# Router of tiles 4 and 5 behind the last output product, one pass of largest values for four tiles, VectorE in program order

## The chip, the core and the metric

The kernel runs on one core of a Trainium2 chip. The time is device microseconds (us) from the start to the end of one execution. TensorE multiplies matrices and transposes by multiplying with an identity; VectorE and ScalarE do the elementwise work; GpSimd (POOL in the rows) does small copies and the indirect gathers; the sync queue (SP) issues nearly all DMAs. In the rows VectorE is DVE, ScalarE is ACT, TensorE is PE, its loads of stationary operands are PEld.

## What is computed

One layer over 1024 tokens of width 1024, in eight tiles of 128 tokens (0 to 7), in float32 throughout: a mixer (differential attention of four heads beside a short convolution, then an output projection), a residual with norms, and an expert-choice mixture of 16 experts. This is the part that matters here:

```python
cap = CAP_FACTOR * t // N_EXPERTS                     # 128 tokens for each expert
logits = einsum('btd,de->bte', x_tok, w_router)       # 16 logits a token
aff = softmax(logits, axis=-1)
g, idx = lax.top_k(swapaxes(aff, 1, 2), cap)          # each expert takes its 128 best tokens of 1024
xs = x_tok[idx]                                       # gathered rows, then SwiGLU of that expert, times g
```

No expert can begin before the scores of all eight tiles are there, since the smallest of its 128 largest scores (the threshold) is needed to pick its tokens.

## The kernel before

**Precision.** A float32 product is made of three products of halves (`mm3`, L166 to L168): ScalarE writes a rounded copy `hi` (L162), VectorE the rest `lo` (L163). Expert weights (`raw`) go through that split too, in loads of 512 KB, 384 in all.

**Order of the work.** The attention runs over 32 steps (L1219). Each step calls `fill(n)`, which issues a few products of convolution and output projection from a generator (`work`, L864), runs functions that are due (`due`), and lets the background sorting go on (`bg`). When a pair of tiles has its last output product (`rests`, L827), its `chain` (L1008) is handed to `due`, function by function, a few calls of `fill` apart (`HK`): scaled, added, square, root, two transposes (`xtr`, L911), logit, gate, the rest of the gate, transposes of the scores (`turn`), their copies (`fourths`). `square` also issues the stores of the tile's rows to `hS`, from which the experts gather, and to `out`. The last pair (tiles 6 and 7) doesn't use `chain`: its steps are written out from L1326 on, after the attention.

**What orders the engines.** The sync queue runs in program order. TensorE does so only at the very start; after that a planner of the language orders TensorE, ScalarE, VectorE and GpSimd by program order as a priority and by its own idea of when operands are ready. Each engine then runs its list strictly in that order.

**Largest values.** For a pair of tiles the 16 scores of each token are transposed (`afft`), so that an expert is a row. `quads` copies four quarters of 64 scores into `sw`, at rows 0, 32, 64 and 96, two of them negated (`SIGN`). `topk` takes the maxima of each quarter, eight at a time (eight times `V.max` and seven times `match_replace`, L968 and L971), which sorts the 64 values; then quarters are merged by `net` (L949), a sorting pass of seven levels with two instructions each, first the two halves, then both against `tops`, the 128 largest of the pairs before. So there is one `topk` for each pair of tiles, and `tops` goes from one to the next. For the last pair no full sort follows: the minimum of the 128 kept is the threshold `thr0`.

**After it** (L1401 on): the threshold is transposed to every partition, copied, and compared with all scores (`ge`); prefix sums on TensorE (`pp`) give each chosen token its place in its expert's list (`pos`); `route(0)` builds the one-hot matrix `oh`, from it the indices, and gathers the rows `xs` (L1439). `chunk(0, 0)` splits the first four weight loads, `xsplit` scales and splits the gathered rows, and the loop over experts (L1496) begins with the products `hg`.

**Pages.** Tiles of 128 x 1024 float32 live in pages: 23 in `pgA` and, once the attention's buffers are free, 7 in `pgX`. Output weights hold 16 of them until the last output products. `load_raw` takes a page for each weight load; the rows `x` and the products `res` of a pair hold pages too, and `res` is used again for the transposed rows in `xtr`. `live` counts the tiles that have rows loaded: `load_x2` may go up to 2, or 4 once all parts have been issued, and `logit` gives two back. `x1` is a pool of the expert stage, with `xs` and `y` in it.

Of the kernel before, what the change touches and what calls it, by code (L numbers as in the profile page):

```python
# [20 lines left out]
P = 128  # L21
# [131 lines left out]
def build(tc, nc, I, out, dbg=None):  # L153
# [17 lines left out]
    with es:  # L171
# [654 lines left out]

        def rests(p):  # L827
            d = {"ss": sm.tile([P, 2], F32, name="ss2")}
            for k in range(2):
                for nh in range(2):  # L830
                    yield from group(2 * p + k, nh, NPT, KT)
                squared(2 * p + k, "res", d["ss"][:, k:k + 1])
            for n, fn in chain(p, d):
                later(n, fn)
# [76 lines left out]
        def xtr(t, g):  # L911
            xT = st[t]["res"].rearrange("p (k e) -> p k e", e=P)
            pp = bank([P, 4, P], "pt4")
            for j in range(4):
                PE.transpose(out=pp[:, j, :], in_=st[t]["x"][:, (4 * g + j) * P:(4 * g + j + 1) * P], identity=ident)
            S.activation(xT[:, 4 * g:4 * g + 4, :], pp, AF.Copy)
# [7 lines left out]
        sw = kp.tile([112, 64], F32, name="sw")  # L924
        sz = [kp.tile([112, P], F32, name=f"sz{i}") for i in range(2)]
# [36 lines left out]
        def topk(p):  # L962
            z0, z1 = sz
            eng = V if p == KT // 2 - 1 else NE[p]
            for r in range(8):

                m = z0[0:112, 8 * r:8 * r + 8]
                V.max(m, sw)  # L968
                yield 1
                if r < 7:  # L970
                    V.match_replace(out=sw, in_to_replace=m, in_values=sw, imm_value=-4.0)  # L971
# [13 lines left out]
            if p < KT // 2 - 1:  # L985
                yield from net(eng, E)
                V.tensor_copy(out=tops, in_=z1[0:E])
                yield 1
            else:
                V.tensor_reduce(out=thr0, in_=z0[0:E], axis=AX.X, op=OP.min)  # L990
# [334 lines left out]

        t6, t7 = KT - 2, KT - 1  # L1326
# [28 lines left out]
        thr = rq.tile([P, E], F32, name="thr")  # L1355
# [5 lines left out]
        while due:  # L1361
            fill(0)
        s2 = sm.tile([P, 2], F32, name="sq2")
# [10 lines left out]
        for _ in range(NR2):  # L1374
            load_raw(pgX if 0 <= nraw[0] - NR0 < NPX else pgA)
        pl = bank([P, 2, E], "pl")
# [16 lines left out]
        pq = [afft(t) for t in (t6, t7)]  # L1393
        for t in (t6, t7):
            quads(t, pq[t - t6])
        bg(1000)
# [6 lines left out]
        V.tensor_copy(out=thr, in_=pth)  # L1403
        thb = thr[:, None, :].to_broadcast([P, KT, E])
# [86 lines left out]

        first = chunk(0, 0)
        cur = route(0)
        xh_, xl_ = xsplit(cur[2], cur[4], V)
        e5.close()
# [108 lines left out]
```

## Time and profile before

| | |
|---|---|
| median of 3 runs | 1399.57 us (1394.0 to 1402.64) |
| profiled execution, own time | 1401.37 us |
| its span | 1399.6 us |
| TensorE busy | 1259.0 us, 90% |
| VectorE busy | 1104.3 us, 79% |
| ScalarE busy | 805.7 us, 58% |
| DMA | 346.67 MB, mean 248 GB/s |

The shares are averages over three kinds of stretch: projections up to about 240 us, attention with output projection up to about 715 us, the router in its last part and up to about 764 us, experts up to about 1355 us, and the sum at the end. The chain that ended last lies for 47% of the span on TensorE and for 8% on VectorE. A row of a timeline gives the start, the duration, the engine, the line, the operation with output and input, their shape, the count of instructions merged in the row, and in brackets the idle time before it with the engine and tile that ended it.

### The profile page before, as it was taken

Reading aid. Unit: us, or ns where it says so; the run is one execution under the profiler, and the core shown is the slowest. Engines: PE = TensorE matmul, PEld = TensorE weight load, DVE = VectorE, ACT = ScalarE, POOL = GpSimd, SP = SyncE. Lnnn points to the kernel's source line nnn. Section 1 sums busy time; section 2 is a strip of 40 time slices with the busy share of each in tenths; the row PEclk is TensorE's granted clock in tenths of the full one; section 3 lists DMA queues with packets and bytes.
Section 4 is the critical chain, followed back from the end, with each engine's and each line's share of the span. In section 5 each row is a group of like instructions: output and inputs, shape, how many; then the busy total and the mean of one; then the engine's idle time right before and its main releaser. Section 6 shows DMA issues by size and latency. Waiting matters only on the chain.

```text
span 1399.6 us, 18794 instructions
## 1 busy us (share of the span) xinstructions
PE 1259.0 (90%) x6457; PEld 1028.7 (73%) x6457; DVE 1104.3 (79%) x2005; ACT 805.7 (58%) x1191; POOL 70.8 (5%) x56
## 2 busy tenths in 40 slices
PE   6999998999989699789762999999999999999990
PEld 3587886887878578677652888888888888877770
DVE  6963666988778667698686799999999998888885
ACT  6632112443434444453331888888888888888762
POOL 0000000000000000000001000000000001201012
PEclk8999999999999899999775999999999999999995
DMA  9359456554486963432287899999999999999736
GB/s 351 117 109 325 133 159 208 162 164 136 142 160 182 235 218 110 136 124 95 76 311 275 278 364 389 374 376 376 379 373 378 377 379 379 354 345 350 267 120 120
DMA packets 143376, 346.67 MB, mean 248 GB/s; under 512 B 17456, under 2 KB 59952, under 8 KB 142640
## 3 DMA queue, kind: packets, MB, share of 16 engines
q1 hardware_dynamic: 115520, 310.34, 63.4%
q0 software_dynamic: 5616, 20.45, 6.1%
q10 hardware_dynamic: 22144, 14.68, 3.7%
q8 instruction: 51, 0.84, 0.2%
q14 instruction: 45, 0.37, 0.1%
HBM read 296.65 MB, written 48.77 MB: 247 GB/s over the span
## 4 chain that ended last, share of the span: by engine, by line
PE 47%; DVE 8%; ACT 2%; issue 1%; DMA 1%; SPq 0%; POOL 0%; POOLq 0%; ACTq 0%; DVEq 0%
PE hg L167 4%; PE hg L168 4%; PE hg L166 4%; PE hu L166 4%; PE hu L167 4%; PE hu L168 4%; PE pyy L167 4%; PE pyy L168 4%; PE pyy L166 4%; PE ptt L1479 2%; PE pl L921 1%; DVE nm L1099 1%; PE ptt L1451 1%; PE pf L799 1%; PE ps L1090 1%
## 5 line engine op out<-in xcount | busy, mean ns | idle before, releaser
L163 DVE TENSOR_TENSOR wlo<-raw,whi 128x1024 fp32r<-128x1024 f32 x384 | 450.1, 1221 | 30.8 <-ACT whi L162 24.5
L162 ACT ACTIVATE whi<-raw 128x1024 fp32r<-128x1024 f32 x384 | 396.1, 1066 | 61.7 <-PE hu L168 24.9
L1103 ACT ACTIVATE e<-ps,nm 128x1280 f32<-128x1280 f32 x64 | 84.4, 1325 | 68.5 <-DVE nm L1099 61.3
L1099 DVE TENSOR_REDUCE nm<-ps 128x1 f32<-128x1280 f32 x64 | 92.8, 1485 | 16.0 <-PE ps L1090 15.9
L167 PE MATMUL pyy<-wlo,ach 128*128 128x512 f32 x256 | 101.3, 396 | 3.5 <-DVE wlo L163 3.1
L166 PE MATMUL hu<-whi,xsh 128*128 128x512 f32 x256 | 101.9, 398 | 0.0
L168 PE MATMUL hg<-whi,xsl 128*128 128x512 f32 x256 | 101.2, 395 | 0.8 <-DVE xsl L163 0.8
L167 PE MATMUL hg<-wlo,xsh 128*128 128x512 f32 x256 | 101.8, 398 | 0.0
L166 PE MATMUL hg<-whi,xsh 128*128 128x512 f32 x256 | 101.3, 396 | 0.0
L167 PE MATMUL hu<-wlo,xsh 128*128 128x512 f32 x256 | 100.8, 394 | 0.0
L168 PE MATMUL pyy<-whi,acl 128*128 128x512 f32 x256 | 100.2, 391 | 0.0
L168 PE MATMUL hu<-whi,xsl 128*128 128x512 f32 x256 | 99.9, 390 | 0.0
L1135 ACT ACTIVATE ath<-ptr 128x512 fp32r<-128x512 f32 (+1 forms) x96 | 47.5, 525 | 90.7 <-PE ptr L1130 90.4
L166 PE MATMUL pyy<-whi,ach 128*128 128x512 f32 x256 | 98.9, 402 | 0.0
L1090 PE MATMUL ps<-KK,q 128*128 128x512 f32 (+1 forms) x384 | 91.0, 384 | 7.8 <-ACT e L1103 6.2
L1090 PEld LDWEIGHTS ps<-KK,q 128*128 128x128 f32 x384 | 65.1, 202 | 18.8 <-ACT e L1103 7.4
L679 PE MATMUL pf<-xh,wl 128*128 128x512 f32 x192 | 77.7, 405 | 0.0
L677 PE MATMUL pf<-xl,wh 128*128 128x512 f32 x192 | 77.3, 403 | 0.0
L675 PE MATMUL pf<-xh,wh 128*128 128x512 f32 x192 | 77.0, 401 | 0.0
L1138 DVE TENSOR_TENSOR atl<-ptr,ath 128x512 fp32r<-128x512 f32 (+1 forms) x96 | 55.6, 596 | 13.8 <-ACT ath L1135 13.6
L167 PEld LDWEIGHTS pyy<-wlo,ach 128*128 128x128 f32 x256 | 48.2, 188 | 18.0 <-DVE wlo L163 8.2
L167 PEld LDWEIGHTS hg<-wlo,xsh 128*128 128x128 f32 x256 | 48.9, 191 | 11.5 <-DVE wlo L163 1.1
(293 smaller groups left out, 2728.8 us busy)
## 6 DMA issues: line engine op xcount, KB each, us to landing
raw<-in_we SPq DMA_DIRECT2D x384, 512.0 KB, 9.5
wa<-in_wa SPq DMA_DIRECT2D x64, 256.0 KB, 4.8
wraw<-in_wF SPq DMA_DIRECT2D x20, 512.0 KB, 6.4
waw<-in_wa SPq DMA_DIRECT2D x16, 512.0 KB, 5.9
q<-qS SPq DMA_DIRECT2D x64, 128.0 KB, 4.9
mS<-hl SPq DMA_DIRECT2D x48, 128.0 KB, 4.2
vS<-hv ACTq DMA_DIRECT2D x20, 256.0 KB, 6.5
KK<-kS SPq DMA_DIRECT2D x16, 320.0 KB, 4.9
```

The source lines that it names most:

```text
L162: S.activation(hi, src, AF.Copy)
L163: eng.tensor_sub(lo, src, f(hi))
L166: PE.matmul(ps, wh, mh, start=first, stop=False)
L167: PE.matmul(ps, wh, ml, start=False, stop=False)
L168: PE.matmul(ps, wl, mh, start=False, stop=last)
L675: PE.matmul(ps, wh[:, kt, :], xh[kt][:, sl], start=first, stop=False)
L677: PE.matmul(ps, wh[:, kt, :], xl[kt][:, sl], start=False, stop=False)
L679: PE.matmul(ps, wl[:, kt, :], xh[kt][:, sl], start=False, stop=last)
L1090: PE.matmul(ps[:, m, k0:k0 + n], q[:, m, j, :], KK[:, m, k0:k0 + n], start=(j == 0), stop=(j == 1))
L1099: V.tensor_reduce(out=c[1][-1], in_=c[0][:, m, :], axis=AX.X, op=OP.max, negate=True)
L1103: S.activation(e, c[0][:, m, :], AF.Exp, bias=c[1][3 + m], accum_out=l[:, m:m + 1])
L1138: V.tensor_sub(x[1], x[2], f(x[0]))
```

## The change

Four edits go together.

1. Of the chain of tiles 4 and 5 only the first four functions (scaled, added, square, root) are handed to `due`. The rest is kept in `held`. Both transposes and the logits (`held[:3]`) are called after the last output products of tiles 6 and 7; the gate in its two parts (`held[3:5]`) after the rows of tiles 6 and 7 have been stored and transposed. The last two, transposes and copies of scores, are not called: `turn2` takes their place. `xtr` puts the transposed rows of tiles 4 and 5 in `xs` and `y` of `x1` and uses other PSUM banks when they are there.
2. `turn2` transposes the scores of two tiles at once (32 rows) and copies two halves of 64 into `sw`. Pair 4, 5 fills rows 0 to 63, pair 6, 7 rows 64 to 127. `topk2` then sorts all four tiles in one pass of eight maxima on 128 rows, merges the halves on 96 rows, then, with a sign for each half (`sgn`), the two tiles of each pair on 32 rows, after a shuffle the two pairs and, on 16 rows, the result with `tops`, and takes the minimum. The `topk` of pair 4, 5 and that of pair 6, 7 go; those of the first two pairs stay.
3. From after the attention to the first `xsplit`, VectorE's instructions stand in program order instead of the planner's. In this stretch `route(0)` now comes ahead of `chunk(0, 0)`.
4. The copy of the threshold from PSUM goes; the comparisons read PSUM.

```diff
--- before.py
+++ after.py
@@ -824,14 +824,19 @@
 
         psE = []
 
+        held = []
+
         def rests(p):
             d = {"ss": sm.tile([P, 2], F32, name="ss2")}
             for k in range(2):
                 for nh in range(2):
                     yield from group(2 * p + k, nh, NPT, KT)
                 squared(2 * p + k, "res", d["ss"][:, k:k + 1])
-            for n, fn in chain(p, d):
-                later(n, fn)
+            for i, (n, fn) in enumerate(chain(p, d)):
+                if p == KT // 2 - 2 and i > 3:
+                    held.append(fn)
+                else:
+                    later(n, fn)
 
         def squared(t, n, to):
             S.activation(st[t]["res"] if n == "x" else page(pgA, "junk"), st[t][n], AF.Square, accum_out=to)
@@ -909,8 +914,10 @@
             SY.dma_start(out=bc[n], in_=bass.AP(tensor=src.tensor, offset=src.offset, ap=[[0, P], [1, D]]))
 
         def xtr(t, g):
+            if t in (KT - 4, KT - 3) and g == 0:
+                st[t]["res"] = x1.tile([P, D], F32, name=("xs", "y")[t % 2])
             xT = st[t]["res"].rearrange("p (k e) -> p k e", e=P)
-            pp = bank([P, 4, P], "pt4")
+            pp = psE[0].tile([P, 4, P], F32, name="pt4", tag="acc") if psE else bank([P, 4, P], "pt4")
             for j in range(4):
                 PE.transpose(out=pp[:, j, :], in_=st[t]["x"][:, (4 * g + j) * P:(4 * g + j + 1) * P], identity=ident)
             S.activation(xT[:, 4 * g:4 * g + 4, :], pp, AF.Copy)
@@ -921,8 +928,12 @@
                 PE.matmul(pl, xT[:, kt, :], wr2[:, kt, :], start=(kt == 0), stop=(kt == KT - 1))
 
 
-        sw = kp.tile([112, 64], F32, name="sw")
-        sz = [kp.tile([112, P], F32, name=f"sz{i}") for i in range(2)]
+        sw = kp.tile([P, 64], F32, name="sw")
+        sz = [kp.tile([P, P], F32, name=f"sz{i}") for i in range(2)]
+
+        sgn = kp.tile([2 * E, 1], F32, name="sgn")
+        V.reduce_sum(sgn, ident[0:2 * E, E:2 * E], axis=AX.X)
+        V.tensor_scalar(sgn, sgn, -2.0, 1.0, op0=OP.mult, op1=OP.add)
         thr0 = kp.tile([E, 1], F32, name="thr0")
         for a in [sw] + sz:
             G.memset(a, -1.0)
@@ -961,14 +972,14 @@
 
         def topk(p):
             z0, z1 = sz
-            eng = V if p == KT // 2 - 1 else NE[p]
+            eng = NE[p]
             for r in range(8):
 
                 m = z0[0:112, 8 * r:8 * r + 8]
-                V.max(m, sw)
+                V.max(m, sw[0:112, :])
                 yield 1
                 if r < 7:
-                    V.match_replace(out=sw, in_to_replace=m, in_values=sw, imm_value=-4.0)
+                    V.match_replace(out=sw[0:112, :], in_to_replace=m, in_values=sw[0:112, :], imm_value=-4.0)
                     yield 1
             for a in (0, 64):
                 neg(z0[a:a + E, 64:P], z0[a + 32:a + 32 + E, 0:64])
@@ -982,12 +993,39 @@
                 yield from net(eng, E, True)
                 V.tensor_tensor(out=z0[0:E], in0=tops, in1=z1[0:E], op=OP.max)
                 yield 1
-            if p < KT // 2 - 1:
-                yield from net(eng, E)
-                V.tensor_copy(out=tops, in_=z1[0:E])
-                yield 1
-            else:
-                V.tensor_reduce(out=thr0, in_=z0[0:E], axis=AX.X, op=OP.min)
+            yield from net(eng, E)
+            V.tensor_copy(out=tops, in_=z1[0:E])
+            yield 1
+
+        def turn2(t):
+
+            pq = bank([2 * E, P], "pq")
+            PE.transpose(out=pq, in_=aff[:, t:t + 2, :].rearrange("p k e -> p (k e)"), identity=ident)
+            for k in range(2):
+                q = t % 4 // 2 * 2 + k
+                V.tensor_scalar(sw[32 * q:32 * q + 2 * E, :], pq[:, 64 * k:64 * k + 64], SIGN[q], None, op0=OP.mult)
+
+        def topk2():
+
+            z0, z1 = sz
+            for r in range(8):
+                m = z0[:, 8 * r:8 * r + 8]
+                V.max(m, sw)
+                if r < 7:
+                    V.match_replace(out=sw, in_to_replace=m, in_values=sw, imm_value=-4.0)
+            n = 2 * E
+            for a in (0, 64):
+                neg(z0[a:a + n, 64:P], z0[a + 32:a + 32 + n, 0:64])
+            run(net(V, 96))
+            neg(z0[0:n], z1[64:64 + n])
+            V.tensor_tensor(out=z0[0:n], in0=z1[0:n], in1=z0[0:n], op=OP.max)
+            V.tensor_scalar(z0[0:n], z0[0:n], sgn[:, 0:1], None, op0=OP.mult)
+            run(net(V, n, True))
+            V.stream_shuffle(z0[0:n], z1[0:n], SWAP)
+            V.scalar_tensor_tensor(z0[0:E], z0[0:E], -1.0, z1[0:E], op0=OP.mult, op1=OP.max)
+            run(net(V, E, True))
+            V.tensor_tensor(out=z0[0:E], in0=tops, in1=z1[0:E], op=OP.max)
+            V.tensor_reduce(out=thr0, in_=z0[0:E], axis=AX.X, op=OP.min)
 
         def gates(ts, pl):
             n = len(ts)
@@ -1323,6 +1361,9 @@
                 tick()
                 assert now[0] < 1000, (stored, sorted(map(str, marks)), len(todo), len(lazy), len(sent), len(hot), due)
 
+        bg(1000)
+        eD = ExitStack()
+        eD.enter_context(tc.manual_schedule(engines={EN.DVE}))
         t6, t7 = KT - 2, KT - 1
 
         def eacc(name):
@@ -1352,7 +1393,6 @@
         x1 = pool(e6, "x1")
         tokb = rq.tile([P, KT, E, 3, 3], BF, name="tokb")
         r8 = rq.tile([P, KT, 3], BF, name="r8")
-        thr = rq.tile([P, E], F32, name="thr")
         pos = rq.tile([P, KT, E], F32, name="pos")
         rest = rq.tile([P, KT, E], F32, name="rest")
         G.tensor_copy(out=tokb[:, :, :, :, 0], in_=late["tok"][:, :, None, :].to_broadcast([P, KT, E, 3]))
@@ -1360,6 +1400,8 @@
             load_raw(pgX if 0 <= nraw[0] - NR0 < NPX else pgA)
         while due:
             fill(0)
+        for fn in held[:3]:
+            fn()
         s2 = sm.tile([P, 2], F32, name="sq2")
         for k, t in enumerate((t6, t7)):
             V.tensor_mul(st[t]["res"], st[t]["res"], bc["G1"])
@@ -1373,6 +1415,9 @@
             SY.dma_start(out=hS[t * P:(t + 1) * P, :], in_=st[t]["x"])
         for _ in range(NR2):
             load_raw(pgX if 0 <= nraw[0] - NR0 < NPX else pgA)
+        for fn in held[3:5]:
+            fn()
+        turn2(KT - 4)
         pl = bank([P, 2, E], "pl")
         for k, t in enumerate((t6, t7)):
             logits(t, pl[:, k, :])
@@ -1390,18 +1435,15 @@
 
         run(gates((t6, t7), pl))
         scale_parts()
-        pq = [afft(t) for t in (t6, t7)]
-        for t in (t6, t7):
-            quads(t, pq[t - t6])
-        bg(1000)
+        turn2(t6)
+        topk2()
         for t in (t6, t7):
             SY.dma_start(out=out[t * P:(t + 1) * P, :], in_=st[t]["x"])
 
 
         pth = bank([P, E], "pth")
         PE.transpose(out=pth, in_=thr0.to_broadcast([E, P]), identity=ident[0:E, 0:E])
-        V.tensor_copy(out=thr, in_=pth)
-        thb = thr[:, None, :].to_broadcast([P, KT, E])
+        thb = pth[:, None, :].to_broadcast([P, KT, E])
         ge = rq.tile([P, KT, 2, E], BF, name="ge")
         V.tensor_tensor(out=ge[:, :, 0, :], in0=aff, in1=thb, op=OP.is_gt)
         V.tensor_tensor(out=ge[:, :, 1, :], in0=aff, in1=thb, op=OP.is_equal)
@@ -1489,9 +1531,10 @@
             V.tensor_mul(a, a, hu)
             return a
 
+        cur = route(0)
         first = chunk(0, 0)
-        cur = route(0)
         xh_, xl_ = xsplit(cur[2], cur[4], V)
+        eD.close()
         e5.close()
         for e in range(E):
             idx, g = cur[:2]
```

## Rows read from the trace of the kernel before

**Rows 1.** Busy time by engine in three stretches, then granted clock, DMA share, GB/s.

```profile
690.00:700.00 10.00, 8.94 (x42) 8.44 (x41) 2.08 (x14) 3.28 (x7) 0.00 (x0) 0.54 0.68 251
...
728.00:736.00 8.00, 7.28 (x48) 6.79 (x48) 7.69 (x34) 5.10 (x10) 0.79 (x4) 0.71 0.93 305
850.00:900.00 50.00, 50.00 (x266) 41.59 (x264) 46.47 (x48) 42.90 (x55) 4.85 (x3) 1.00 1.02 373
```

**Rows 2.** Waits of the sync queue from 675 us: total us, times, longest.

```profile
SPq L845 <- DVE wlo L163: 375.2, 315, 24.2
```

**Rows 3.** Timeline of TensorE, 686 to 700 us.

```profile
686.77 0.40 PE L803 MATMUL pf<-woh,mB 128*128 128x512 f32 x1
...
693.19 6.84 PE L921 MATMUL pl<-wr,res 128*128 128x16 f32 x32
699.87 0.77 PE L799 MATMUL pf<-woh,mA 128*128 128x512 f32 x1
```

**Rows 4.** Timeline of TensorE, attention products to the last logits.

```profile
701.30 0.41 PE L166 MATMUL po<-ath,vv 128*128 128x256 f32 x1
...
704.46 0.28 PE L166 MATMUL po<-ath,vv 128*128 128x256 f32 x1
...
706.12 0.28 PE L168 MATMUL po<-ath,vv 128*128 128x256 f32 x1
...
713.19 0.60 PE L1334 MATMUL px<-ones,sq 128*128 128x1 f32 x4
...
727.86 3.88 PE L915 MATMUL pt<-ident,xr 128*128 128x128 f32 x16 [11.15 <-DVE xr L1369]
731.54 3.73 PE L921 MATMUL pl<-wr,res 128*128 128x16 f32 x32
```

**Rows 5.** Timeline of VectorE: roots, gates, residual, copies, maxima, sorting levels.

```profile
685.24 0.16 DVE L197 TENSOR_SCALAR nz<-ss 128x2 f32<-128x2 f32 x1
...
687.61 2.48 DVE L1020 SCALAR_TENSOR_TENSOR xr<-res,nz,xr 128x1024 f32<-128x1024 f32 x2
...
700.07 0.38 DVE L996 SCALAR_TENSOR_TENSOR rlg<-pl,rr,cst 128x16 f32<-128x16 f32 x2 [5.96 <-PE pl L921]
...
701.63 0.37 DVE L1006 TENSOR_SCALAR aff<-rex,rsx 128x16 f32<-128x16 f32 x2
...
717.40 2.73 DVE L1346 SCALAR_TENSOR_TENSOR res<-pf,nz,res 128x512 f32<-128x512 f32 x4
...
726.45 2.46 DVE L1369 SCALAR_TENSOR_TENSOR xr<-res,nz,xr 128x1024 f32<-128x1024 f32 x2
...
735.31 0.38 DVE L996 SCALAR_TENSOR_TENSOR rlg<-pl,rr,cst 128x16 f32<-128x16 f32 x2 [0.31 <-PE pl L921]
...
739.17 0.45 DVE L945 TENSOR_SCALAR sw<-pq 16x64 f32<-16x64 f32 x2
...
741.57 0.23 DVE L968 MAX8 sz<-sw 112x8 f32<-112x64 f32 x1
...
745.17 0.22 DVE L956 TENSOR_TENSOR sz<-sz 80x64 f32<-80x64 f32 x1
...
748.47 0.21 DVE L956 TENSOR_TENSOR sz<-sz 16x64 f32<-16x64 f32 x1
...
751.15 0.28 DVE L983 TENSOR_TENSOR sz<-tops,sz 16x128 f32<-16x128 f32 x1
```

**Rows 6.** VectorE, TensorE timelines; weight splits (page); landing of all gathers.

```profile
740.99 0.43 DVE L1410 CAST tokb<-rest 128x128 bf16<-128x128 f32 x1
...
754.91 0.42 DVE L1424 SCALAR_TENSOR_TENSOR pc<-pp,ge 128x256 f32<-128x256 f32 x1 [2.09 <-PE pp L1421]
...
763.59 3.75 PE L1479 MATMUL ptt<-dgx,xs 128*128 128x128 f32 x16 [5.82 <-DMA xs<-hS,idx]
...
L163 DVE TENSOR_TENSOR wlo<-raw,whi 128x1024 fp32r<-128x1024 f32 x384 | 450.1, 1221 | 30.8 <-ACT whi L162 24.5
...
DMA to landing us min/median/max: 4.4/8.2/12.0
```

## The prediction

> **What bounds the kernel now.** I began with the share of busy time and the slices of the page, then read the stretches one by one. In the expert stage TensorE is the bound: in fifty of its microseconds the engine is busy for all fifty at full clock, with VectorE and ScalarE below it [rows 1]. The weight loads are on time: the sync queue stands for 375 us in all for pages that VectorE has still to free [rows 2], so it runs as far ahead as its pages allow. Whatever starts the first expert earlier therefore moves everything behind it by as much; a microsecond saved ahead of 764 us is a microsecond of the run.
>
> Ahead of it two stretches stand out on TensorE. **First hole:** the output products of the last tile stop with the one at 686.77 and go on at 699.87 [rows 3]. Between them TensorE has only the transposes and router logits of tiles 4 and 5; the logits alone take 6.84 us, at a granted clock of 0.54 [rows 1, 3]. They come in that order because the chain of that pair is emitted there. The products behind them want nothing of it. **Second hole:** after the last output product TensorE idles 11.15 us, until 727.86 [rows 4], because VectorE is working through residual and norm of tiles 6 and 7. From there the chain of waits is VectorE's nearly alone: router of tiles 6 and 7, then the sorting passes, to 754.91, then the gather of the first expert, which TensorE awaits at 763.59 [rows 5, 6].
>
> **The change, part by part.**
>
> *a. Router of tiles 4 and 5 leaves the first hole.* It issues no DMA: the stores of those tiles' rows belong to an earlier step that stays. From the end of the product at 686.77 (the next would start 0.40 later, at 687.17) to 699.87 are 12.70 us [rows 3]. What follows was also slow because the clock was still down: from 701.30 to 704.46 are 15 of the 30 attention products, 3.16 us; 14 more from 704.46 to 706.12 take 1.66 us, 0.119 each [rows 4]. At that pitch the first 15 take 1.78, so 1.38 less. Three output products there, 699.87 to 701.30, take 1.43 instead of 0.70: 0.73 less. Small things are left in this stretch: two transposes of scores and a wait for VectorE's sorting of that pair, an estimate of 0.5 us. Together 15.3 us at the four small products of 713.19. From there to the first residual step at 717.40 lie 4.21 us [rows 4, 5], in which a 12-step root is interleaved with sorting; the same kind of root alone took 2.37 us, from 685.24 to 687.61 [rows 5]. With 0.6 + 0.46 us of matmul and wait in front (estimates from the small products' 0.60) I take 3.4 us: 0.8 less. Sum a: **16.1 us**. Bounds: 12.7 if the clock gives nothing back, 16.5 above.
>
> What could be late next: the input rows of tiles 6 and 7 are loaded when the last parts are issued, and not after the logits any more; they wait for two pages, which the squares of tiles 4 and 5 free near 691 us, and they are wanted only near 707. The rows of tiles 4 and 5 hold two of 23 pages some 15 us longer, so two of the first weight loads take others; the pages of output weights come free with the last products, which are earlier too. I cost that at nothing; without this cover it is rival B.
>
> *b. It goes into the second hole.* From the last product to the first transpose of tile 6 are about 9.4 us (11.15 less the 1.75 of the next step). To be put there: 16 transposes and 32 passes of logits, 3.88 + 3.73 = 7.6 us by the rows of tiles 6 and 7 [rows 4], or 4.5 + 6.84 = 11.3 at half clock, the 4.5 an estimate (16 at the 0.28 us to which 0.14 us of full clock doubles). So nothing if the clock holds, about 2 us if it does not. I take nothing.
>
> *c. Residual and norm of tiles 6 and 7.* VectorE's program order takes the sorting and the early weight splits out of the way. From 717.40 to the second half of the residual at 726.45 are 9.05 us [rows 5]. Four residual adds, two products and the root alone are 2.64 + 2.28 + 2.37 = 7.3 (first two by that stretch without the sorting, third by the root above): 1.75 us less. Then gates of tiles 4 and 5 (1.93 us, from 700.07 to the end at 702.00 [rows 5]), transpose and two copies (about 1.0) and a root (2.37) stand in front of the gates of tiles 6 and 7: 5.3 us on VectorE, with ScalarE's exponents waited for in the middle. In the kernel before, the same gates come 735.31 - 728.84 = 6.47 us after that residual, when the logits end [rows 4, 5]. So VectorE is just hidden by TensorE. I take **1.5 us** gained; bounds +2.6 (logits earlier) and -4.1 (rival A).
>
> *d. Gates and copies of the last pair.* From 735.31 to the end of the last copy at 739.62 are 4.31 us; gates alone 1.93, one transpose instead of two and two copies instead of four about 1.05: **1.3 us** gained, bounds 1.0 and 1.5.
>
> *e. Largest values of four tiles in one pass.* The shape grows from 112 to 128 rows; a sorting level costs the same at 80 rows (745.17 to 747.9, 2.74 for seven) as at 16 (748.47 to 751.15, 2.68), so rows are free [rows 5]. Before: 739.62 to 751.15, 11.53 us. After: two rounds of 0.59 undisturbed, then 3.60 (741.57 to 745.17), 3.30 (to 748.47), one more sorting pass on 32 rows at 2.68, three more small instructions (sign, shuffle, maximum) at about 0.28 each, and the last pass of 2.68: 14.28 us. So **2.75 us lost**; bounds 2.4 and 3.3, by the small instructions' spread of 0.2 to 0.45. The whole pass over tiles 4 and 5 that this replaces gives nothing more: it ran beside other work and is counted in a, c and d.
>
> *f. Threshold and casts.* The copy of the threshold goes: 0.2 gained. Five casts and differences of the gate values (0.43 the longest [rows 6], some 2.2 in chain) now stand between the comparisons and the product at 754.91, where VectorE was idle 2.09 us for TensorE [rows 6]: 0.1 lost, 2.2 if that cover is gone.
>
> *g. Splits of the first weights.* Four of 1.22 us [rows 6] come behind the first gather instead of ahead of it. The gather is what TensorE waits for, 5.82 us in its row [rows 6], and 4.9 us of splits fit into it: nothing, or up to 4.9 without that cover. But they free pages while the gather is under way, and weight loads then share the DMA engines with it: a gather landed in 4.4 us at best, 8.2 in the middle, 12.0 at worst over the run [rows 6], and the first is at the low end. I charge **1.0 us**, nearer to the row of the first; bounds 0 and 6.8.
>
> **Sum:** 16.1 + 1.5 + 1.3 - 2.75 + 0.2 - 0.1 - 1.0 = 15.25 us. The profiled execution took 1401.37 us (span 1399.6), 1.8 above the median of the three runs: 1386.1 against itself, 1384.3 against the median. I say 1385.
>
> **Rivals.**
>
> *A. The clock stays down in the tail: about 1390.* The held logits run at half clock and so push the transposes of tiles 6 and 7, whose logits are then slow as well. Place: TensorE from the last product to the gates. Transposes 4.5 and logits 6.84 twice over give gates 22 us after the first residual step instead of 17.9: the 1.5 of c becomes -4.1, so the gain is about 9.7. For it: the first hole did run at 0.54 [rows 1]. Against: in the second, the logits behind 16 transposes ran at 3.73 us, full pace, the clock averaging 0.71 over that stretch [rows 1, 4]. The Trainium skill (TensorE: Matmul & The Clock Gate, Part 4: PE-mode transpose) says that transposes do not count as work for the clock, so a run of them would leave it at half; this trace disagrees with it where it matters, since the clock had come back by the logits behind them. By that rule the sum would be this rival's. Chance 0.14.
>
> *B. Loads and gather, or an uncovered split: about 1390 to 1393.* If the weight stream starts later against the earlier router, or the splits outlast the gather, g costs 6 to 7 us instead of 1. For: the stream has to find pages. Against: 30 pages, and the queue waits for pages, not for data. Chance 0.12.
>
> *C. Slower: about 1404.* The held transposes and logits are not put into the second hole but behind the rows of tiles 6 and 7, since TensorE's order is the planner's. Their 12.7 us come back on the tail; the longer sorting (2.75) and, in program order, the splits (4.9) are then paid as well: 16.1 + 1.5 - 12.7 - 2.75 - 4.9 - 1 = about -4. It decides by whether the transposes of tile 4 stand before or after those of tile 6. Against: they want only rows that are ready long before. Chance 0.06.
>
> *D. It does not do what it says: about 1400.* The planner leaves the hole where it was, another wait taking its place at 687 us. Nothing in the rows holds the attention products there. Chance 0.06.
>
> **How the numbers follow.** Forecast 0.62, its own range 1381 to 1389 (bounds of a, c and e). For 8 in 10 the range takes in A and most of B, and the scatter of the runs shown, 1394.0 to 1402.6: 1379 to 1393. One per cent, about what a measurement of this kernel tells from no change, is 14.0 us, at 1385.6, hard by the forecast: somewhat over half of the forecast's chance and a little beyond it lies under that, 0.40; A, B, D and the rest of the forecast give 0.54; C gives 0.06.
>
> **What would show it.** Right: in the profile after, attention products follow the output products without logits between; the last output product ends 15 us earlier; transposes and logits of tiles 4 and 5 lie before those of tile 6; one pass of eight maxima with 128 rows where there were two, some 14 us long; the first gather 5 us. Wrong: logits of 6.8 us in the tail (A), a gather over 8 us or splits behind its landing (B), a VectorE idle for TensorE's score transposes (c), or an idle TensorE still near 687 us (D).

## The result, and the profile after

The changed kernel takes 1386.87 us (median of 6 runs, 1377.18 to 1390.24) against 1401.11 us of the kernel before (6 runs, 1394.0 to 1408.44): ratio 0.9895, 95% interval 0.9854 to 0.9937. Run again later, beside the kernel before on another occasion, it took 1382.54 us, ratio 0.9891 (0.9860 to 0.9922). The forecast of 1385 was met, but by a sum in which one step had the wrong sign and a gain that was not in the sum made up for much of it. That part is luck.

The profiled execution of the changed kernel took 1390.24 us (span 1388.5), so against [rows 1 to 6] it is 11.1 us faster, less than the medians differ (14.2). I follow it from the last norm transposes in the attention (tile `pr`) on; they stand at 678.86 us before and at 682.01 after. These 3.15 us arose earlier and are scatter: in a second execution of the changed kernel `pr` stands at 676.40, and over the profiled executions of all kernels below it lies anywhere from 672.4 to 682.7 us. From there to the first expert product are 89.03 us before (767.89 - 678.86) and 77.95 after (759.96 - 682.01): **11.08 us** gained. From there to the end of the run are 633.48 and 630.28: **3.2 us** more. 11.08 + 3.2 - 3.15 = 11.13.

Timeline of TensorE after, from the output products to the first expert; it answers to [rows 3, 4] and to TensorE's line in [rows 6]:

```profile
690.02 0.40 PE L803 MATMUL pf<-woh,mB 128*128 128x512 f32 x1
690.25 0.40 PE L799 MATMUL pf<-woh,mA 128*128 128x512 f32 x1
...
700.79 0.50 PE L1375 MATMUL px<-ones,sq 128*128 128x1 f32 x4
...
704.02 1.94 PE L922 MATMUL pt<-ident,xr 128*128 128x128 f32 x16
705.80 1.86 PE L928 MATMUL pl<-wr,xs 128*128 128x16 f32 x16
...
708.84 1.06 PE L928 MATMUL pl<-wr,y 128*128 128x16 f32 x8 [0.29 <-ACT y L923]
713.37 3.65 PE L922 MATMUL pt<-ident,xr 128*128 128x128 f32 x16 [3.46 <-DVE xr L1411]
718.88 0.39 PE L1003 MATMUL pq<-ident,aff 128*32 128x128 f32 x1 [1.87 <-DVE aff L1044]
719.07 6.85 PE L928 MATMUL pl<-wr,res 128*128 128x16 f32 x32
...
755.66 3.60 PE L1521 MATMUL ptt<-dgx,xs 128*128 128x128 f32 x16 [5.91 <-DMA xs<-hS,idx]
...
759.96 0.50 PE L166 MATMUL hg<-whi,xsh 128*128 128x512 f32 x1
```

The last product of one group of output products and the first of the next follow 0.23 us apart, where 13.1 us lay between them [rows 3]. Transposes and logits of tiles 4 and 5 stand in the second hole, and they are quick: 1.94 us for 16 transposes. But two lines are new. The transposes of tiles 6 and 7 are followed by 1.87 us in which TensorE waits for the scores of tile 4, and the logits behind that take 6.85 us, as slow as those that had left the attention.

Windows after: bounds, length, busy time of the five engines, granted clock, DMA share, GB/s; they answer to [rows 1]:

```profile
688.00:700.00 12.00, 12.00 (x68) 10.44 (x67) 8.24 (x32) 4.25 (x8) 0.00 (x0) 1.00 0.61 220
704.00:710.00 6.00, 5.61 (x49) 5.34 (x47) 5.36 (x9) 5.34 (x10) 0.00 (x0) 1.00 1.03 413
712.00:717.00 5.00, 3.63 (x16) 3.27 (x16) 2.89 (x5) 3.70 (x7) 0.00 (x0) 0.50 1.03 410
719.00:726.00 7.00, 6.92 (x33) 6.81 (x32) 2.46 (x16) 1.11 (x2) 1.81 (x6) 0.50 1.03 415
850.00:900.00 50.00, 50.00 (x266) 41.80 (x265) 44.99 (x46) 43.99 (x62) 3.21 (x2) 1.00 1.02 388
```

The clock is full through the old hole and through the held router. It falls near 711.2, while TensorE waits for the rows of tiles 6 and 7, and is still at half when their logits end. Two more timelines follow: of VectorE, which answers to [rows 5, 6], and of ScalarE where VectorE waits for it:

```profile
704.10 2.73 DVE L1387 SCALAR_TENSOR_TENSOR res<-pf,nz,res 128x512 f32<-128x512 f32 x4
...
714.34 0.37 DVE L1034 SCALAR_TENSOR_TENSOR rlg<-pl,rr,cst 128x16 f32<-128x16 f32 x2
...
718.25 0.17 DVE L1042 RECIPROCAL rsx<-rsx 128x2 f32<-128x2 f32 x1 [3.33 <-ACT rex L1040]
...
725.96 0.38 DVE L1034 SCALAR_TENSOR_TENSOR rlg<-pl,rr,cst 128x16 f32<-128x16 f32 x2 [3.85 <-PE pl L928]
...
728.92 0.23 DVE L1013 MAX8 sz<-sw 128x8 f32<-128x64 f32 x1
...
743.31 0.28 DVE L1027 TENSOR_TENSOR sz<-tops,sz 16x128 f32<-16x128 f32 x1
...
746.88 0.42 DVE L1466 SCALAR_TENSOR_TENSOR pc<-pp,ge 128x256 f32<-128x256 f32 x1
...
751.32 4.62 DVE L163 TENSOR_TENSOR wlo<-raw,whi 128x1024 fp32r<-128x1024 f32 x4
```

```profile
713.25 1.06 ACT L842 ACTIVATE res<-xr 128x1024 f32<-128x1024 f32 x1 [2.58 <-DVE xr L1411]
...
714.45 1.06 ACT L842 ACTIVATE res<-xr 128x1024 f32<-128x1024 f32 x1
...
715.50 2.14 ACT L923 ACTIVATE res<-pt 128x512 f32<-128x512 f32 x4
717.54 0.30 ACT L1040 ACTIVATE rex<-rlg,rmx 128x16 f32<-128x16 f32 x1
```

The gates of tiles 4 and 5 need ScalarE's exponents (`rex`). ScalarE does the squares and copies of tiles 6 and 7 first, from 713.25 to 717.64, so VectorE waits 3.33 us; the transpose of those scores waits for VectorE; and the logits of 6 and 7 stand behind that transpose in TensorE's list. The sync queue's waits for pages are what they were, 390.1 us in 328 waits against 375.2 [rows 2].

### The profile page after: what moved, and what is told of

It is laid out like the page before. It is cut to its first block, busy times and chain, and to the rows that moved or that the text cites. A ratio compares the mean times of both kernels' runs of the same rounds, so it can differ in the third digit from the quotient of the medians.

```text
span 1388.5 us, 18732 instructions
## 1 busy us (share of the span) xinstructions
PE 1254.7 (90%) x6455; PEld 1026.4 (74%) x6455; DVE 1099.7 (79%) x1950; ACT 805.2 (58%) x1191; POOL 71.8 (5%) x56
## 4 chain that ended last, share of the span: by engine, by line
PE 43%; DVE 9%; DMA 3%; ACT 2%; issue 2%; POOL 0%; POOLq 0%; DVEq 0%; ACTq 0%
PE hg L167 4%; PE hg L168 4%; PE hg L166 4%; PE hu L166 4%; PE hu L167 4%; PE hu L168 4%; PE pyy L167 4%; PE pyy L168 4%; PE pyy L166 3%; DMA raw<-in_we 3%; PE ptt L1521 2%; DVE wlo L163 2%; DVE nm L1137 1%; PE pl L928 1%; PE pf L799 1%
## 5 line engine op out<-in xcount | busy, mean ns | idle before, releaser
L675 PE MATMUL pf<-xh,wh 128*128 128x512 f32 x192 | 76.5, 398 | 0.0
L1176 DVE TENSOR_TENSOR atl<-ptr,ath 128x512 fp32r<-128x512 f32 (+1 forms) x96 | 55.5, 595 | 13.1 <-ACT ath L1173 12.9
```

The source lines that it names most:

```text
L675: PE.matmul(ps, wh[:, kt, :], xh[kt][:, sl], start=first, stop=False)
L1176: V.tensor_sub(x[1], x[2], f(x[0]))
```

## The experiments

The measure that does not hang on the scatter ahead is a stretch of the profiled execution: from `pr`, or from the four small products `px` behind it, to the first expert product. From `px` it is 54.70 us before and 59.17 after (59.02 in the second profile); `pr` to `px` is 34.33 and 18.78 (17.91). Of the kernels below all but the third hold `pr` to `px` at 17.9 to 18.7 us. The kernel before took 1397.84 us in the first four comparisons, 1397.35 in the next four and 1397.66 in the last three. Only the last three had the changed kernel beside them; in the others times are compared with it by their ratio to the kernel before. Edits are shown shortened.

**Held router alone.** On the kernel before:

```diff
+                if p == KT // 2 - 2 and i > 3: held.append(fn)
+        for fn in held[:3]: fn()      # behind the last output products
+        for fn in held[3:]: fn()      # ahead of the logits of 6 and 7
```

> The kernel before with the first edit alone: the router of tiles 4 and 5 comes behind the last output product; each pair keeps its own sorting, and VectorE stays with the planner. Before, from the last norm transposes in the attention (pr) to the first expert product (hg) are 89.0 us, in the changed kernel 78.0; from pr to the four small products px 34.3 and 18.8. My theory: the hole in TensorE goes with this edit alone, so pr to px is 18.8 (18 to 20); but without the common pass the whole sorting of pair 4, 5 (some 11 us) lands on the tail, in front of that of pair 6, 7, and takes back most of it: pr to hg 85 to 88, time 1395 to 1400. Rival (the common pass only tidies up, and the sorting of pair 4, 5 is hidden): pr to hg 76 to 80, time as the changed kernel's.

Measured: `pr` to `px` 17.96, `pr` to the first expert product 81.37 us, time 1385.61, ratio 0.9925 (0.9898 to 0.9952). The hole goes with this edit alone. My range of 85 to 88 was missed, and so was the rival's of 76 to 80: my price for the second sorting pass was too high, and the rival's too low: the maxima of tiles 6 and 7 begin 12.8 us after their logits are used, not the 3.0 of the changed kernel, but much of the pass of 4 and 5 still ran beside the slow stretch ahead. My time was wrong by 9 us or more; 6.4 us of that were gained behind the first expert product (627.1 us to the end, against 633.5), nearly all of it in four late experts; see the last experiment on those.

**VectorE back with the planner** (in the changed kernel):

```diff
-        eD = ExitStack()
-        eD.enter_context(tc.manual_schedule(engines={EN.DVE}))
...
-        eD.close()
```

> The changed kernel without the third edit: VectorE is ordered by the planner again between the attention and the first expert. My theory: program order on VectorE is worth little; gates of 4 and 5 may come earlier on TensorE's list, the wait of 3.3 us for their exponents shrinks, and a few small costs (weight splits between the sorting) come back: pr to hg 76 to 80, time within 3 us of the changed kernel's. Rival (program order carries a good part of the gain, since the planner puts weight splits of 1.22 us and other work on the tail's path): pr to hg 83 or more, time 1392 or more.

Measured: 75.00 us from `pr`, 57.07 from `px`, time 1379.99, ratio 0.9864 (0.9843 to 0.9885). The program order carries none of the gain; in this stretch it costs 2 us (57.07 us from `px` against 59.17 and 59.02), a little more than my range of 76 to 80 from `pr` allowed. TensorE here:

```profile
711.92 0.40 PE L1003 MATMUL pq<-ident,aff 128*32 128x128 f32 x1 [2.23 <-DVE nz L209]
713.91 3.64 PE L922 MATMUL pt<-ident,xr 128*128 128x128 f32 x16 [1.59 <-DVE xr L1409]
717.35 4.12 PE L928 MATMUL pl<-wr,res 128*128 128x16 f32 x32
```

The planner puts the gates of 4 and 5 between the steps of the root, so their scores are transposed ahead of the rows of 6 and 7, nothing stands between transposes and logits, and the logits take 4.12 us. Against the run with the held router alone, `px` to the first expert product is 57.07 instead of 63.41. The two differ by the common pass with its transposes of two tiles at once, by the direct threshold, and by the place of `route(0)` ahead of the weight splits. From the transpose of the threshold to the first expert product they take 16.5 and 16.1 us, so the 6.3 us lie ahead of it, where the common pass is.

**Router of 4 and 5 back in the attention** (common pass and program order kept):

```diff
-                if p == KT // 2 - 2 and i > 3: held.append(fn)
-                else: later(n, fn)
+                if p < KT // 2 - 2 or i < 9: later(n, fn)
...                                    # xtr as in the kernel before
```

> The changed kernel with the first edit undone: transposes, logits and gates of tiles 4 and 5 are back at their place in the attention; one pass sorts four tiles, and VectorE stays in program order. My theory: the hole in TensorE comes back (pr to px 33 to 35), the longer sorting stays and nothing pays for it: pr to hg 88 to 92, time 1398 to 1404, as before or slower. Rival (the gain comes from the common pass or from VectorE's order, and the hole was hidden): pr to hg 82 or less, time below 1392.

Measured: `pr` to `px` 33.35, `pr` to the first expert product 87.67, time 1399.51 (10 runs), ratio 1.0008 (0.9990 to 1.0027). The hole is back, with logits of 6.85 us at 696.09, and the gain is gone (my range for the stretch was 88 to 92). The first edit is the necessary one.

**Exponents of 4 and 5 ahead of the rows of 6 and 7:**

```diff
         r = rsqrt(ss, D, 2)
+        held[3]()
...
-        for fn in held[3:5]: fn()
+        held[4]()
```

> The changed kernel with one call moved: the first half of the gates of tiles 4 and 5 (logits, maximum, exponents) stands right behind the root of tiles 6 and 7, ahead of their normalised rows, so that ScalarE does the exponents before the squares and copies of those rows. In the changed kernel VectorE waits 3.33 us for these exponents, and the transpose of the scores of tile 4 stands on TensorE ahead of the logits of 6 and 7. My theory: the wait falls below 0.5 us, the logits of 6 and 7 begin as soon as their transposed rows are there, 1 to 2 us earlier, and the gates 2 to 3 us earlier against the last transposes of rows: pr to hg 75 to 76.5, time 1 to 3 us less. Rival (the logits at the low clock alone, 6.85 us, set the gates): pr to hg changes by under 0.5 us.

Measured: 72.86 us from `pr`, 54.28 from `px`, so 4.8 us less than the changed kernel; time 1381.90, ratio 0.9884 (0.9859 to 0.9908), which can't be told from the changed kernel's 0.9895 and 0.9891. ScalarE, then TensorE:

```profile
708.56 0.31 ACT L1040 ACTIVATE rex<-rlg,rmx 128x16 f32<-128x16 f32 x1 [1.77 <-DVE rmx L1036]
...
709.75 1.06 ACT L842 ACTIVATE res<-xr 128x1024 f32<-128x1024 f32 x1 [0.50 <-DVE xr L1412]
```

```profile
709.86 3.65 PE L922 MATMUL pt<-ident,xr 128*128 128x128 f32 x16 [3.84 <-DVE xr L1412]
713.30 0.42 PE L1003 MATMUL pq<-ident,aff 128*32 128x128 f32 x1
713.51 3.84 PE L928 MATMUL pl<-wr,res 128*128 128x16 f32 x32
```

The exponents now lie in ScalarE's idle time, VectorE's wait for them is gone, and the same logits behind the same half-clock transposes take 3.84 us. The gain in the stretch was more than I had expected (75 to 76.5 us), since the logits now run at full clock as well. The next two runs part the two.

**Scores of 4 and 5 transposed behind the logits of 6 and 7**, exponents left where they were:

```diff
-        turn2(KT - 4)
         pl = bank([P, 2, E], "pl")
         for k, t in enumerate((t6, t7)):
             logits(t, pl[:, k, :])
+        turn2(KT - 4)
```

> The changed kernel with the call that transposes and copies the scores of tiles 4 and 5 moved behind the logits of 6 and 7. So TensorE no longer waits for those scores between the last transposes of rows and the logits; the exponents of 4 and 5 stay behind squares and copies on ScalarE, and VectorE still waits for them. In the changed kernel TensorE idles 1.87 us there and the logits take 6.85 us at half clock; with the exponents called first these were 0 and 3.84. My theory: the idle TensorE kept the clock down, so without it the logits take 3.7 to 4.5 us; gates of 6 and 7 then come from VectorE's side, 2.5 to 4.5 us earlier, and from the last norm transposes to the first expert product are 74 to 75.5 us instead of 77.95. Rival (the order of ScalarE's exponents and squares sets the clock and the gates, TensorE's wait being only a sign of it): logits still 6 us or more, and 77 us or more.

Measured: logits 3.85 us, 75.05 us from `pr`, 57.11 from `px`; time 1380.19, ratio 0.9882 (0.9850 to 0.9914). The logits and the stretch are as forecast; the gates come 2.3 us earlier counted from `px`, just under my 2.5 (3.1 from `pr`, of which 0.85 arose ahead of `px`).

```profile
706.18 3.65 PE L922 MATMUL pt<-ident,xr 128*128 128x128 f32 x16 [3.46 <-DVE xr L1411]
709.62 3.85 PE L928 MATMUL pl<-wr,res 128*128 128x16 f32 x32
713.33 0.27 PE L1003 MATMUL pq<-ident,aff 128*32 128x128 f32 x1
718.77 0.39 PE L1003 MATMUL pq<-ident,aff 128*32 128x128 f32 x1 [5.17 <-DVE aff L1044]
```

The logits end 5 us before the next scores come: now VectorE, still behind the exponents, is what is late. The clock in windows, up to the end of the transposes and from there to the end of the logits:

```profile
706.20:709.90 3.70, 3.70 (x18) 3.70 (x19) 1.50 (x4) 3.66 (x8) 0.00 (x0) 0.50 1.03 410
710.10:713.40 3.30, 3.30 (x31) 3.29 (x31) 0.54 (x3) 2.83 (x7) 0.00 (x0) 1.00 1.02 408
```

It rose within 0.3 us of the end of the transposes.

**The 1.87 us filled:**

```diff
+        wm = eacc("wm")
+        for _ in range(3):
+            PE.matmul(wm[:, 0:256], st[t6]["res"][:, 0:P], st[t6]["res"][:, 0:256], start=True, stop=True)
         for fn in held[3:5]: fn()
```

> The changed kernel with three more float32 products of 128x256, never read, between the transposes of the rows of 6 and 7 and that of the scores of 4 and 5: they keep TensorE at work in the 1.87 us in which it waits for the scores, and change no order and no operand. My theory: the clock comes up, the logits take 3.7 to 4.5 us instead of 6.85, and the stretch from the last norm transposes to the first expert product is 75 to 76.5 us. Rival (the clock comes up only behind a longer stretch of work, or the idle time has no part in it): logits 6 us or more, stretch 77.5 to 79.

Measured: 74.97 us from `pr`, 57.04 from `px`; time 1378.21, ratio 0.9847 (0.9815 to 0.9878).

```profile
707.41 3.65 PE L922 MATMUL pt<-ident,xr 128*128 128x128 f32 x16 [3.47 <-DVE xr L1411]
710.85 1.98 PE L1420 MATMUL wm<-res 128*128 128x256 f32 x6
712.92 0.28 PE L1003 MATMUL pq<-ident,aff 128*32 128x128 f32 x1
713.04 4.78 PE L928 MATMUL pl<-wr,res 128*128 128x16 f32 x32
```

The clock in windows, in the transposes and the first half of the three products, from there into the logits, and in their last part:

```profile
707.50:711.80 4.30, 4.30 (x19) 4.12 (x20) 1.43 (x4) 4.26 (x10) 0.00 (x0) 0.50 1.03 410
712.00:715.20 3.20, 3.10 (x26) 2.66 (x24) 2.26 (x14) 2.16 (x4) 0.00 (x0) 1.00 1.02 407
715.40:717.80 2.40, 2.40 (x12) 2.31 (x11) 0.53 (x4) 0.00 (x0) 1.34 (x6) 0.50 1.03 418
```

Work that nobody reads, in place of idle time, shortens the logits from 6.85 to 4.78 us and the stretch from `px` by 2.1 us. The windows show how: the clock rose near 711.9, within the three products, and fell again near 715.3, with the last third of the logits still to run. So my range of 3.7 to 4.5 us for the logits was missed. Transposes or products with no gap behind them brought the clock up; the logits alone did not, in 6.85 us of work without a break in the changed kernel, nor in the 6.84 us of the first hole [rows 3]. The idle TensorE is what kept the clock down between the transposes and the logits, but the logits do not hold it up either. With the run before: of the 4.8 us that the exponents' place is worth, some 2 are the logits' clock (59.1 to 57.1 from `px`) and some 2.8 VectorE's wait (57.1 to 54.28).

> The changed kernel with the three filling products between the transposes of the rows of 6 and 7 and that of the scores, once more and beside the two others of this call. My theory: 0.984 to 0.988 of before, and 3 to 6 us under the changed kernel: 3 by the stretch up to the first expert product, up to 2.6 by a first expert that starts at a higher clock. Rival (the first result was the scatter of few runs): within 2 us of the changed kernel.

Measured in this second run: logits 4.83 us, 75.73 us from `pr`, 57.11 from `px`; time 1381.10, ratio 0.9883 (0.9851 to 0.9915), 1.4 us under the changed kernel beside it. The stretch from `px` repeats, and so does the fall of the clock within the logits; the first time of 1378.21 was partly scatter, and for the whole run the rival was right (within 2 us).

**The gap of 3.8 us filled.** On the kernel with the exponents first, without the three products; the second kernel has the four `wg` as well ("the kernel before" at the start of its text is the first of the two):

```diff
         for fn in held[:3]: fn()
+        for _ in range(7): PE.matmul(wm[:, 0:256], y5[:, D - P:D], y5[:, D - 256:D], ...)   # y5: st[KT - 3]["res"]
...
         cur = route(0)
+        for _ in range(4): PE.matmul(wg[:, 0:256], cur[4], iota2, ...)
```

> The kernel with the exponents of 4 and 5 called first, and seven float32 products of 128x256, never read, behind the logits of 4 and 5, where TensorE idles 3.8 us. With the exponents first alone, the transposes of the rows of 6 and 7 took 3.65 us at half clock, the logits behind them 3.84, and the stretch from the last norm transposes to the first expert product 72.86. My theory: the clock stays up over the gap, transposes about 2 us, and the gates come 0.5 to 1.8 us earlier, as far as ScalarE's squares and copies of those rows allow: stretch 71 to 72.4. Rival (the transposes let the clock fall, so that the logits are slow behind them): transposes 2 us, logits 5 us or more, stretch 73 or more.

> The kernel before with, beside those seven products, four more that are never read behind the building of the first gather's indices, in TensorE's wait of 5.8 us for the gathered rows. My theory: transposes of the gathered rows and the first expert products run at full clock sooner, worth 1 to 3 us behind the gather (from those transposes to the second hidden product), and the whole is the fastest version, 0.984 to 0.988 of the kernel before. Rival (the clock falls again in the rest of the gather wait, or the products stand in the way of the next expert's positions): no gain against the version with seven products, or a loss of up to 1 us.

Measured: with seven, transposes of 6 and 7 in 1.91 us, logits 3.75, 71.93 us from `pr`, 53.33 from `px`; time 1380.82, ratio 0.9870 (0.9841 to 0.9899). With both, 70.68 and 52.75 us; 1383.09, ratio 0.9890 (0.9866 to 0.9914). The stretch shortens as the theory said; with both, from the transposes of the gathered rows to the second hidden product are 3.93 us instead of 4.89, the low end of my 1 to 3. The time does not follow: from the first expert product to the end are 632.4 and 634.1 us, against 630.8 with the exponents first alone. In the first of them the expert began at half clock for 8 us (749.79 to 757.85) and took 2.8 us longer; in the second it took 0.6 longer, and most of the loss lies in the late experts, where VectorE's list had come out otherwise (next experiment). So the second forecast (fastest version) was wrong; what filling is worth by itself these two do not show.

**Where the late experts wait.** One line of TensorE's timeline in the kernel before, the same product in the changed kernel, and VectorE's lines that lead to the first of them:

```profile
1238.23 0.50 PE L167 MATMUL pyy<-wlo,ach 128*128 128x512 f32 x1 [2.48 <-DVE wlo L163]
```

```profile
1226.13 0.50 PE L167 MATMUL pyy<-wlo,ach 128*128 128x512 f32 x1 [0.42 <-DVE wlo L163]
```

```profile
1235.21 1.23 DVE L1430 TENSOR_TENSOR oh<-iota,pos 128x1024 bf16<-128x1024 f32 x1 [1.61 <-PE pi L1435]
1236.35 0.68 DVE L163 TENSOR_TENSOR xsl<-xsy,xsh 128x512 fp32r<-128x512 f32 x1
1236.95 2.35 DVE L163 TENSOR_TENSOR wlo<-raw,whi 128x1024 fp32r<-128x1024 f32 x2
```

In the kernel before, the one-hot matrix of a later expert stands ahead of the weight splits, waits for TensorE, and TensorE then waits 2.48 us for the splits. VectorE's lists differ there from build to build, although no edit touches the expert loop: that order is in the lists of the kernel before, of the router put back, of the exponents first and of the kernel with both `wm` and `wg`, and their traces have one wait of 2.47 or 2.48 us (in the last of them an expert earlier); it is in none of the others, whose longest wait in the late experts is 0.75. The wait is not all of it. From the first product of the twelfth expert to that of the sixteenth are 151.9 us in the kernel before and 149.8 in the changed one, but 145.7 with the router held alone; two executions of one build agree within 0.1 (149.8 and 149.7 for the changed kernel).

Two runs on that, the changed kernel as it is, and the exponents first with `range(2)` in the loop of `wm` above:

> The changed kernel, unchanged, beside the kernel before on the same chip. My theory of the part behind the first expert product: of the 3.2 us that the changed kernel gained there, some 2.3 come from VectorE's list in the late experts, where the planner put the one-hot matrix of the next expert ahead of two weight splits in the kernel before (TensorE waits 2.5 us once) and not in the changed one. That list is fixed when the kernel is built, so this run shows no wait of over 0.5 us there again; the ratio comes out at 0.988 to 0.993. Rival (the wait is an accident of one execution): it may appear here as well.

> The kernel with the exponents of 4 and 5 called first, with two float32 products of 128x256, never read, behind the logits of 4 and 5: too few to fill the gap of 3.8 us, but with them the planner's list for VectorE in the late experts comes out without the one-hot matrix ahead of the splits. My theory: up to the first expert product nothing changes much (72.0 to 73 us from the last norm transposes, against 72.86), the wait of 2.5 us in the late experts goes, and from the first expert product to the end are 627.5 to 629 us instead of 630.8, or up to 632 if the first expert starts at half clock for 8 us; time 0.985 to 0.987 of before. Rival (the weight stream is what makes TensorE wait there, because the experts start earlier than it does): the wait stays at 2 to 3 us or moves to an earlier expert.

Measured: the changed kernel again, no wait over 0.42 us there, 76.93 us from `pr`, time 1382.54. The kernel with two products: longest wait 0.45 us, 72.19 us from `pr`, 54.28 from `px`, 629.3 us behind (0.3 more than I had set); time 1378.42, ratio 0.9865 (0.9833 to 0.9897). The wait comes with the list that the build fixes, not with the weight stream, since here the experts start earlier than with the exponents first alone (744.56 against 751.18) and it is gone. Only part of it is gained: those four experts take 151.7 us, against 153.3 with the wait, as the twelfth gives back 1.2. This is the fastest of the last comparison, 4.1 us under the changed kernel; the intervals of the two overlap.

## Why the prediction was right, and where it was wrong

By its own steps, in the two profiled executions:

| step | forecast | measured | from |
|---|---|---|---|
| a, first hole | +16.1 | +16.45 | `pr` to first residual step, 38.54 to 22.09 |
| b, second hole | 0 | 0 | held router 704.02 to 709.90 at full clock, then 3.46 idle |
| c, residual to gates | +1.5 | **-3.95** | 17.91 to 21.86 |
| d, gates and copies | +1.3 | +1.35 | 4.31 to 2.96 |
| e, one pass | -2.75 | -2.86 | 11.53 to 14.39 |
| f, threshold, casts | +0.1 | +0.19 | 3.76 to 3.57 |
| g, gather | -1.0 | -0.10 | 12.98 to 13.08 |
| sum | +15.25 | +11.08 | |

**a, b, d, e and f** were right in place and size, and the router put back shows that a carries the gain. **g** was overcharged: four splits of 4.62 us, from 751.32 on, end 0.3 us behind the gather, which kept TensorE waiting 5.91 us against 5.82 [rows 6].

**c failed, in sign.** The sentence was "So VectorE is just hidden by TensorE". I had seen that ScalarE's exponents were waited for, but costed no ScalarE time in front of them, and I let the logits follow the transposes without asking what the new transpose of scores between them waits for. The loss is that of rival A, -4.1, and in A's place, and the sign that the prediction gave for A, logits of 6.8 us in the tail, is there. But the first link of A did not happen: the held logits did not run at half clock and pushed nothing (and 16 transposes at half clock took 3.65 us, not the 4.5 of its estimate). What happened is a chain through three engines, squares and copies on ScalarE, gates on VectorE, scores on TensorE, and then the clock. Moving one call gives 4.8 us back, which is most of the 5.45 between forecast and measurement: with the exponents first the step takes 17.18 us (700.21 to 717.39), a gain of 0.7. The rest I did not part further.

The Trainium skill (TensorE: Matmul & The Clock Gate, Part 4: PE-mode transpose), by whose rule transposes do not count as work for the clock, was the case for A. The runs speak against it here as the trace of before did: the clock holds for transposes too, 16 of which take 1.94 us at full clock and 3.65 at half, and it rises behind them: in the run with the scores behind the logits TensorE had been idle for 3.46 us, ran 16 transposes at a granted clock of 0.50, and had 1.00 within 0.3 us of their end. Where 16 at half clock are followed by the logits with no gap over 0.03 us, these take 3.73 to 4.44 us, against 6.85.

**What was not in the sum** made the median agree. Behind the first expert product 3.2 us were gained. 1.4 came in the first expert (38.7 us instead of 40.1): in the kernel before it begins at half clock, for 8 us up to 776.0, in the changed one it runs at half for 3.4 us (762.35 to 765.80). The next ten experts take the same within 0.2. 2.1 came in the four experts that follow, where the late wait is 2.06 us shorter. None of this was forecast, and the second part hangs on how VectorE's list came out in each build. "A microsecond saved ahead of 764 us is a microsecond of the run" held only within these few microseconds. Rivals B, C and D did not occur: the wait for the gather grew by 0.09 us, the transposes of tile 4 stand before those of tile 6, and TensorE has no hole at 687 us.

## What to carry to other kernels

When work is put into an idle stretch of one engine, follow its whole chain through the other engines' lists: here the moved products were free, but the small steps behind them were queued behind 4.4 us of ScalarE's work and ahead of the next products. A program order written for one engine fixes only that engine; the calls have to stand in an order that serves all three, or the planner does better. And compare stage by stage from a mark in the trace: runs of one kernel, and late waits that a planner moves from build to build, shift the total by up to as much as such a change (single runs of the changed kernel went from 1377.18 to 1390.24 us).

## What was not expected of the hardware

A gap of under 2 us kept TensorE at half clock: after 16 transposes at half clock, logits that follow at once take 3.8 us, with 1.87 us of idle time between 6.85, with that time filled by unread products 4.78. And 32 logit products in a row did not raise the clock in 6.85 us. Eight maxima took 0.23 us on 128 partitions as on 112, a sorting instruction 0.20 to 0.22 on 96, 32 and 16, so the 2.86 us that the pass over four tiles takes more come from its added merge, not from its rows. A comparison whose operand lies in PSUM took 0.29 us, as with one in SBUF.
